# A two-layer encoder: where the memory keys are rounded first, which third of a group turns first, and in which order the last FFN unit multiplies

## The chip, the cores and the metric

The kernel runs on one core of one Trainium2 chip, as one launch. Its time is the device time of an execution in microseconds (us). The engines are named as in the profile: PE is TensorE (matmul and transpose by matmul), DVE is VectorE, ACT is ScalarE, POOL is GpSimd, and SP is SyncE, which here only issues DMA transfers. Each engine works through its own list of instructions strictly in order, and an instruction waits until what it reads and overwrites is free. A wait on one engine therefore also holds up everything behind it on that engine.

## The reference

A trunk of two layers on a sequence of 1,024 tokens with 1,024 channels, and 256 memory tokens, in float32:

```
mem_n = rmsnorm(mem, mem_norm_g)
for layer in (0, 1):
    u      = rmsnorm(h, norm_g[layer, 0])
    mem_kv = mem_n @ w_mem_kv[layer]
    if layer == 0:   # window attention: 16 query heads, 4 key/value heads of 64 channels,
                     # rotary, blocks of 128 tokens see one block to each side, a sink per head
        y = mixer_window_attn(u, mem_kv, a_w_in, a_sink, a_w_out, pos)
    else:            # a gated linear recurrence in both directions, 8 heads
        y = mixer_hgrn2(u, mem_kv, b_w_in, lb_fwd, lb_bwd, b_norm_g, b_w_out)
    # both mixers also hold 4 cross heads of 128 channels into mem_kv,
    # and project [own heads | cross heads] with one output matrix
    h = h + rmsnorm(y, norm_g[layer, 1])
    v = rmsnorm(h, norm_g[layer, 2])
    gate, up = split(v @ ffn_w_in[layer], 2)               # 1024 -> 2 x 2816
    f = (gelu(dwconv3(gate) + conv_b) * up) @ ffn_w_out[layer]
    h = h + rmsnorm(f, norm_g[layer, 3])
```

## The kernel before

Every float32 product is made of three matmuls on rounded halves: an operand x is kept as a rounded part xh and a rest xl, and the kernel adds xh·yh, xl·yh and xh·yl in PSUM (lines 81 to 83 in the mixers, line 555 in the FFN). Making the two parts is called `split`: ACT copies x to xh with rounding (line 86), then DVE subtracts xh from x (line 87). Where a weight is split the same pair stands at lines 76 and 77.

**Layer 0's mixer** works group by group, four groups g of four query heads with one key/value head. `proj(g)` projects eight tiles of 128 tokens (`token`, PE product `pj`, 24 matmuls each). DVE multiplies the result by the rotary cosines and sines (lines 278 and 279), ACT and DVE write the value `v` (lines 283 and 291). In group 0 the call also brings in three rows of the input, whose sums of squares ACT takes (line 290). `turn(b, ...)` transposes one half (four tiles) of queries and keys on PE into the PSUM tile `ptq` (line 303): three transposed parts w, of which w = 0 and 1 are queries (ACT lines 311 and 313, DVE 312 and 314 write `qs`) and w = 2 is the keys (ACT writes `kh` at line 86, DVE `kl` at line 87). `ptq` is one PSUM bank, so a part is transposed after the one before has been read.

`attend(g, ...)` then runs over eight blocks of 128 queries. For each of four heads PE makes scores `ps` from `qs` with `kh` and `kl` (lines 355 and 356), DVE adds the mask and takes the maximum (line 358), ACT takes the exponential (line 365). The last exponential of block n of group g is kept as `marks[g, n]`. After that the probabilities are scaled, transposed (`pt`, line 381), split (`ph`, `pl`) and multiplied with v (`po`, lines 384 and 385). Blocks 0 to 2 need only the first half of the keys, block 3 is the first that needs the second.

`cross_head(0, h, ...)` brings the memory keys and values of one cross head from DRAM into `kvl` (DMA on SP, line 186), and splits them into `kvh` and `kvl`. `cross_unit` uses them on PE, first at 162.7 us in the profiled execution.

After the fourth group the output projection starts. `wo0.begin` (line 420) reads the first heads' results back as `ul`, splits them (ACT line 449, DVE line 450) and multiplies by half of the output weights (`pb`, copied to `y0` by ACT at line 482). For tokens 6 and 7 the ACT copies of the read are held behind a mark:

```
wo0.begin(psq, ("pj", "pj", "ptq"), [...], {6: marks[3, 1], 7: marks[3, 1]})
```

**The FFN** of each layer multiplies in units of 128 hidden channels, f = 0 to 21. The 1,024 tokens are two halves; gate and up for two halves come from seven products instead of eight, numbered 1 to 7, each 12 matmuls (four steps of three). PSUM banks X, V and Y collect them: products 6, 7 and 4 are added one after the other to the same bank X, and before each next one ACT has to copy what X holds (`su`, then half `tj` of `g`, then half `ti` of `g`). Likewise V holds product 5 (copied to `s5`) and then 5 + 3. The right operands u6, u7 and u4 are made once for each layer by `operands()`, while `first_units` computes units 0 to 2. Unit 21 is made by `last_unit` (lines 711 to 732), which calls `ahead()` four times to load and split operands of the next stage, the second product of the FFN.

**What sets the order.** Nothing in the source is an explicit list: the program is given to a scheduler at build time, which orders every engine's instructions by priorities that follow the source. `tc.high_priority(AHEAD)` moves work up, and `tc.issue_after(x)` keeps the instructions within it behind the instruction x. A small edit therefore can move instructions at places that it does not name.

Of the kernel before, what the change touches and what calls it, by code (L numbers as in the profile page):

```python
# [8 lines left out]
F32 = mybir.dt.float32  # L9
# [4 lines left out]
ALU = mybir.AluOpType  # L14
# [4 lines left out]
P = 128  # L19
T = 1024  # L20
D = 1024
NT = T // P
# [22 lines left out]
AHEAD = 2000  # L45


def build(tc, A, out):
    nc = tc.nc
    act, dve, pool, pe = nc.scalar, nc.vector, nc.gpsimd, nc.tensor  # L50
# [18 lines left out]
    def wunit(src, n=1024, pl=None, eng=None):  # L69

        tg = ("wh", "wl") if pl is None else ("xwh", "xwl")
        h = (pl or ring).tile([P, 1024], F32R, tag=tg[0], name=tg[0])
        l = (pl or ring).tile([P, 1024], F32R, tag=tg[1], name=tg[1])
        raw = stg.tile([P, 1024], F32, tag="st", name="st")[:, :n]
        nc.sync.dma_start(raw, src)
        act.copy(h[:, :n], raw)  # L76
        (eng or dve).tensor_tensor(l[:, :n], raw, h[:, :n].bitcast(F32), op=ALU.subtract)  # L77
        return h, l
# [6 lines left out]
    def split(h, l, src):  # L85
        act.copy(h, src)  # L86
        dve.tensor_tensor(l, src, h.bitcast(F32), op=ALU.subtract)  # L87
# [91 lines left out]
                nc.sync.dma_start(kvd[l][:, :, 1, t * P:(t + 1) * P].rearrange("h p d -> p h d"),  # L179
                                  vm[:, t, :].rearrange("p (h d) -> p h d", h=4))  # L180

    def cross_head(l, h, wp):
        kvh = wp.tile([P, 2, 256], F32R, tag="kvh", bufs=1, name="kvh")
        kvl = wp.tile([P, 2, 256], F32R, tag="kvl", bufs=1, name="kvl")
        raw = kvl.bitcast(F32)
        nc.sync.dma_start(raw, kvd[l][h])
        split(kvh, kvl, raw)
        return *wunit(A["wxq"][l, h]), kvh, kvl

    def cross_unit(l, h, b, head, wp, tags, w0, pair):  # L190
# [44 lines left out]
    def window():  # L235
        ea = tc.alloc_tile_pool(name="attn0", bufs=1, reuse_waits="tile")
        ap_ = tc.alloc_tile_pool(name="attn", bufs=2, side="right", reuse_waits="tile")
        psq = tc.alloc_tile_pool(name="aps0", bufs=1, space=PSUM, reuse_waits="tile")
# [10 lines left out]
        xhead = [None]  # L249
# [6 lines left out]
        def proj(g):  # L256
# [5 lines left out]
            v = kvp.tile([P, NT, P], F32R, tag="v", bufs=1, name="v")  # L262
# [31 lines left out]

            def turn(b, rqs):
                hs = slice(b * 512, (b + 1) * 512)
                for w in range(3) if g or b else (2, 0, 1):
                    if g or b or w == 2:
                        tp = psq.tile([P, 4, P], F32, tag="ptq", bufs=1, name="ptq")
                    else:  # L300
                        tp = psp.tile([P, 4, P], F32, tag="pt", bufs=2, name="ptq")
                    for tt in range(4):
                        pe.transpose(tp[:, tt, :], rqs[tt][:, w * P:(w + 1) * P], ident)
                    tp = tp.rearrange("p a b -> p (a b)")
                    if w == 2:
                        split(kh[:, hs], kl[:, hs], tp)
                    else:
                        lo, hi = slice(0, 64), slice(64, 128)
                        q0, q1 = [ap_.tile([P, 512], F32R, tag="qs", bufs=8, name="qs") for _ in range(2)]
                        qs[2 * w][b], qs[2 * w + 1][b] = q0, q1  # L310
                        act.copy(q0[lo], tp[lo])
                        dve.tensor_tensor(q0[hi], tp[lo], q0[lo].bitcast(F32), op=ALU.subtract)
                        act.copy(q1[hi], tp[hi])
                        dve.tensor_tensor(q1[lo], tp[hi], q1[hi].bitcast(F32), op=ALU.subtract)
# [14 lines left out]
        marks, moved = {}, []  # L329
# [7 lines left out]
        def attend(g, qkv, blocks=range(NT)):  # L337
            qs, kh, kl, v = qkv
            for b in range(2):
                for nn in range(4):  # L340
# [5 lines left out]
                    o = pairs[0]  # L346
                    lo, hi = max(n - 1, 0), min(n + 2, NT)
                    w = (hi - lo) * P
# [55 lines left out]
                for _ in range(XU[g][b]):  # L404
                    xh_, xb_ = units.pop(0)
                    if xb_ == 0:
                        xhead[0] = cross_head(0, xh_, ea)
                    cross_unit(0, xh_, xb_, xhead[0], ap_, tags, ea, pair)

        dve.tensor_scalar_mul(sk8, sk, 8.0)  # L410
# [4 lines left out]
        ea.release()  # L415
        tables.release()
        attend(3, cur)
        wo0.open()
        y0 = wo0.w1.tile([P, NT, 512], F32, bufs=1, name="y0")
        wo0.begin(psq, ("pj", "pj", "ptq"), [y0[:, t, :] for t in range(NT)], {6: marks[3, 1], 7: marks[3, 1]})  # L420
        psp.release()
        ap_.release()

# [125 lines left out]
    def mmk(o, n, st, mv, first):  # L549

        for k in range(n):
            (ah, al), (bh, bl) = st(k), mv(k)
            new, end = first and k == 0, k == n - 1
            for x, y, e in ((ah, bh, False), (ah, bl, False), (al, bh, end)):
                pe.matmul(o, x, y, start=new, stop=e, skip_group_check=not first)  # L555
                new = False

    def ffn(l, wo, dst, gnext, halves_, out_halves):
        u2p = tc.alloc_tile_pool(name=f"u2{l}", bufs=1, reuse_waits="tile")
# [10 lines left out]
        ti, tj = hs(i), hs(j)  # L570
# [20 lines left out]
        def gtile():  # L591
            return fp.tile([P, T], F32, tag="g", bufs=1, name="g")
# [25 lines left out]
        def operands():  # L618

            xs = [fp.tile([P, 2, 512], F32, tag="c", bufs=3, name="c") for _ in range(2)]  # L620
            tmp = lambda: fp.tile([P, 2, 512], F32, tag="tt", bufs=2, name="tt")
            half = lambda x, kk: x[:, 2 * kk:2 * kk + 2]
            def more(o, x, part, kk, op):
                for c in range(2):
                    dve.tensor_tensor(o, x, half(part[c], kk).bitcast(F32), op=op)
                    x = o
            def out_of(sp, k, kk, x):
                sp(half(B[k][0], kk), half(B[k][1], kk), x)
            for kk, x in enumerate(xs):
                q = tmp()  # L630
                f32 = lambda t, c: half(t[c], kk).bitcast(F32)
                dve.tensor_tensor(x, f32(B[1], 0), f32(B[5], 0), op=ALU.subtract)
                dve.tensor_tensor(q, f32(B[1], 1), f32(B[5], 1), op=ALU.subtract)
                dve.tensor_tensor(x, x, q, op=ALU.add)
            for kk, x in enumerate(xs):
                out_of(split, 5, kk, x)
            yield
            for kk, x in enumerate(xs):
                more(x, x, B[3], kk, ALU.add)
                out_of(nsplit, 6, kk, x)  # L640
            yield
            for kk, x in enumerate(xs):
                q = tmp()
                more(q, x, B[1], kk, ALU.subtract)
                out_of(split, 7, kk, q)
            yield
            for kk, x in enumerate(xs):
                more(x, x, B[2], kk, ALU.subtract)
                out_of(split, 4, kk, x)
            yield  # L650
# [30 lines left out]
        def prod(k, w, ps, first):  # L681
            wh, wl = w
            bh, bl = B[k]
            mmk(ps, 4, lambda x: (wh[:, x * P:(x + 1) * P], wl[:, x * P:(x + 1) * P]),
                lambda x: (bh[:, x, :], bl[:, x, :]), first)


        oi, oj = (hs(b) for b in out_halves)
# [22 lines left out]
        def last_unit(w, x, v, y, s1, ahead):  # L711
            u = fp.tile([P, T], F32, tag="u", bufs=1, name="u")
            su = fp.tile([P, 512], F32, tag="su", bufs=1, name="su")
            s5 = fp.tile([P, 512], F32, tag="s5", bufs=1, name="s5")
            g = gtile()
            prod(6, w(6), x, False)
            act.copy(su, x)
            prod(2, w(2), y, True)
            dve.tensor_tensor(u[:, ti], y, s1, op=ALU.add)
            ahead()  # L720
            prod(7, w(7), x, False)
            act.copy(g[:, tj], x)
            prod(5, w(5), v, True)
            act.copy(s5, v)
            dve.tensor_tensor(g[:, tj], g[:, tj], s5, op=ALU.add)
            ahead()
            prod(4, w(4), x, False)
            act.copy(g[:, ti], x)
            ahead()
            prod(3, w(3), v, False)  # L730
            dve.tensor_tensor(u[:, tj], v, su, op=ALU.add)
            ahead()
            hidden(NF - 1, conv(NF - 1, g, u))

# [155 lines left out]
        y = {q: yp.tile([P, 4, 512], F32, name=q) for q in ("c11", "c21", "c12", "c22")}  # L890
# [5 lines left out]
        def rows(b, t):  # L896

            if gnext or b == ia:
                x = np_.tile([P, D], F32, tag="x", bufs=4 if gnext else 2, name="x")
            else:  # L900
                x = stg.tile([P, D], F32, tag="st", name="st")
            nc.sync.dma_start(x, h1d[l][tok(b, t), :])
            return x
# [31 lines left out]
        for k in SECOND:  # L935
            if k == 5:
                Xs = left()
            ps = Vs if k == 2 else Xs
            hold = []
            for p in range(NP2):  # L940
                while len(made) < 1:
                    second_ahead()
                h, l_ = made.pop(0)
# [5 lines left out]
                if k == 5 and p in (1, 3, 5, 7):  # L949
                    t = p // 2  # L950
                    tail(ia, t, y["c11"][:, t, :], ss["q11"][:, t:t + 1], y["c21"][:, t, :], ss["q21"][:, t:t + 1], rows(ia, t))
            if k == 3:
                last = [rows(ib, t) for t in range(4)]
            for t in range(4):
                if k in (1, 6, 7, 4):
                    act.copy(y[{1: "c11", 6: "c12", 7: "c22", 4: "c21"}[k]][:, t, :], ps[t])  # L956
                elif k in (2, 5):
                    q = y[{2: "c11", 5: "c22"}[k]][:, t, :]
# [461 lines left out]
    wo0 = Out(0, A["x"], "wout0", list(range(NT)))  # L1420
# [96 lines left out]
```

## Time and profile before

| | before |
|---|---|
| runs (us) | 2664.05, 2664.63, 2672.4; median 2664.63 |
| profiled execution | 2668.36 us, span 2666.4 us, granted clock 0.998 |
| PE busy | 2601.3 us, 98% of the span, 14,420 matmuls |
| DVE, ACT, POOL busy | 1813.5, 1378.9 and 473.7 us (68%, 52%, 18%) |
| end chain | PE 79%, DVE 12%, DMA 3%, ACT 3% |

A row of the timeline is: start, duration of one entry, engine, line, operation, output and input tiles, shape, count; in square brackets stands how long the engine was idle before it and what ended that. Matmuls overlap, so the time a matmul costs is the distance to the next one's start, not the duration shown. A row of waits is: who waited, for whom, microseconds in total, how many times, the longest. In the table by stretches the columns are the stretch, its length, the busy time of PE, PEld, DVE, ACT and POOL with counts, the granted PE clock, the share of DMA time and GB/s.

### The profile page before, as it was taken

What the parts mean: (1) busy time and instruction counts of PE and PEld (TensorE: products, weight loads), DVE (VectorE), ACT (ScalarE), POOL (GpSimd) and SP (SyncE); (2) the same over time, 40 slices, a digit from 0 to 9 for tenths busy, and PEclk for the clock granted to TensorE, in tenths of its full rate; (3) what the DMA queues carried; (4) which work ended last, traced back from release to release, by engine and by line L of the source; (5) the groups of instructions that cost most, each with busy time, mean ns of one, the idle gap of its engine ahead of it and who ended that gap; (6) DMA issues with size and microseconds to landing.
All of it is one profiled execution on the core that took longest, in us unless ns stands there. A gap on an engine that the chain in (4) does not pass through costs nothing.

```text
span 2666.4 us, 39108 instructions
## 1 busy us (share of the span) xinstructions
PE 2601.3 (98%) x14420; PEld 2185.9 (82%) x14420; DVE 1813.5 (68%) x3043; ACT 1378.9 (52%) x2503; POOL 473.7 (18%) x519
## 2 busy tenths in 40 slices
PE   8899999999999999999999999999999999999998
PEld 7888887788888887887888878888788788888887
DVE  6688786578655565478688686887757755656447
ACT  6477666445444444454455554555534444444443
POOL 0331010211111100031224131231211111110013
PEclk9999999999999999999999999999999999999999
DMA  9692232367777857674235251103436778774666
GB/s 353 232 190 54 74 97 72 109 184 194 198 203 192 210 145 258 192 249 154 83 110 149 81 125 56 52 25 96 140 125 176 188 200 210 197 206 158 224 191 237
DMA packets 195728, 425.93 MB, mean 160 GB/s; under 512 B 20048, under 2 KB 56272, under 8 KB 189904
## 3 DMA queue, kind: packets, MB, share of 16 engines
q1 hardware_dynamic: 161840, 325.11, 37.9%
q0 software_dynamic: 24544, 90.19, 16.3%
q10 hardware_dynamic: 9152, 8.14, 1.0%
q8 instruction: 113, 1.85, 0.3%
q14 instruction: 79, 0.65, 0.1%
HBM read 330.04 MB, written 116.39 MB: 167 GB/s over the span
## 4 chain that ended last, share of the span: by engine, by line
PE 79%; DVE 12%; DMA 3%; ACT 3%; issue 1%; POOL 1%; SPq 0%; ACTq 0%; DVEq 0%; POOLq 0%
PE X L555 28%; PE V L555 11%; PE pj L81 6%; PE pj L82 5%; PE pj L83 5%; PE Y L555 5%; PE pb L81 4%; PE pb L83 3%; PE pb L82 3%; DVE E L1139 1%; PE pt L381 1%; DVE wl L77 1%; DVE ER L1174 1%; DMA kvl<-kvd 1%; PE po L1242 1%
## 5 line engine op out<-in xcount | busy, mean ns | idle before, releaser
L87 DVE TENSOR_TENSOR wl<-st,wh 128x1024 fp32r<-128x1024 f32 (+1 forms) x238 | 262.8, 1111 | 325.3 <-ACT wh L86 285.2
L86 ACT CAST wh<-st 128x1024 fp32r<-128x1024 f32 (+1 forms) x238 | 222.5, 937 | 293.8 <-PE X L555 196.2
L81 PE MATMUL pj<-uh,wh 128*128 128x512 f32 x512 | 203.3, 397 | 3.7 <-DVE q L1084 2.0
L555 PE MATMUL X<-wl,wh 128*128 128x512 f32 x528 | 204.7, 389 | 0.0
L555 PE MATMUL X<-wh,wl 128*128 128x512 f32 x528 | 204.6, 389 | 0.0
L82 PE MATMUL pj<-ul,wh 128*128 128x512 f32 x512 | 201.7, 394 | 0.1
L83 PE MATMUL pj<-uh,wl 128*128 128x512 f32 x512 | 201.4, 394 | 0.0
L555 PE MATMUL X<-wh 128*128 128x512 f32 x528 | 198.7, 390 | 1.6 <-ACT c L956 1.6
L81 PE MATMUL pj<-wh,uh 128*128 128x384 f32 (+1 forms) x512 | 190.3, 373 | 9.4 <-DVE cos L1324 5.3
L82 PE MATMUL pj<-wl,uh 128*128 128x384 f32 (+1 forms) x512 | 187.2, 366 | 0.0
L83 PE MATMUL pj<-wh,ul 128*128 128x384 f32 (+1 forms) x512 | 187.1, 366 | 0.0
L77 DVE TENSOR_TENSOR wl<-st,wh 128x1024 fp32r<-128x1024 f32 (+1 forms) x92 | 117.4, 1281 | 28.9 <-ACT wh L76 28.3
L555 PE MATMUL V<-uh,wh 128*128 128x512 f32 x344 | 133.8, 389 | 0.0
L555 PE MATMUL V<-ul,wh 128*128 128x512 f32 x344 | 133.8, 389 | 0.0
L555 PE MATMUL V<-uh,wl 128*128 128x512 f32 x344 | 133.8, 389 | 0.0
L76 ACT CAST wh<-st 128x1024 fp32r<-128x1024 f32 (+1 forms) x98 | 98.9, 1015 | 46.6 <-PE pj L82 25.2
L555 PEld LDWEIGHTS X<-wh 128*128 128x128 f32 x528 | 99.1, 188 | 22.5 <-ACT c L956 2.0
L555 PEld LDWEIGHTS X<-wl,wh 128*128 128x128 f32 x528 | 99.1, 188 | 20.6
L555 PEld LDWEIGHTS X<-wh,wl 128*128 128x128 f32 x528 | 99.1, 188 | 20.6
L81 PEld LDWEIGHTS pj<-uh,wh 128*128 128x128 f32 x512 | 96.3, 188 | 24.0 <-DVE q L1084 2.9
L81 PEld LDWEIGHTS pj<-wh,uh 128*128 128x128 f32 x512 | 96.6, 189 | 21.0 <-issue 5.5
L925 POOL TENSOR_TENSOR c<-c,g 128x512 f32<-128x512 f32 x24 | 43.8, 1844 | 392.4 <-PE X L555 163.0
(399 smaller groups left out, 7211.5 us busy)
## 6 DMA issues: line engine op xcount, KB each, us to landing
st<-hid SPq DMA_DIRECT2D x154, 256.0 KB, 3.1
st<-in_ffw_dram SPq DMA_DIRECT2D x108, 256.0 KB, 3.2
w2s<-in_ffw_dram POOLq DMA_DIRECT2D x24, 1024.0 KB, 8.5
st<-in_ffw_dram SPq DMA_DIRECT2D x46, 512.0 KB, 4.2
hid<-tt SPq DMA_DIRECT2D x88, 256.0 KB, 4.7
st<-w2s SPq DMA_DIRECT2D x88, 256.0 KB, 3.2
sx<-in_ffw_dram SPq DMA_DIRECT2D x84, 256.0 KB, 4.0
sy<-in_ffw_dram SPq DMA_DIRECT2D x42, 512.0 KB, 6.9
```

The costliest lines, as they stand in the source:

```text
L76: act.copy(h[:, :n], raw)
L77: (eng or dve).tensor_tensor(l[:, :n], raw, h[:, :n].bitcast(F32), op=ALU.subtract)
L81: pe.matmul(o, ah, bh, start=first, stop=False)
L82: pe.matmul(o, ah, bl, start=False, stop=False)
L83: pe.matmul(o, al, bh, start=False, stop=last)
L86: act.copy(h, src)
L87: dve.tensor_tensor(l, src, h.bitcast(F32), op=ALU.subtract)
L381: pe.transpose(tp[:, j, :], sm[:, j, c * P:(c + 1) * P], ident)
L555: pe.matmul(o, x, y, start=new, stop=e, skip_group_check=not first)
L925: pool.tensor_tensor(y[q][:, t, :], y[q][:, t, :], g3[:, c], op=ALU.mult)
L1139: dve.tensor_tensor_scan(B[:, rev], smask, a_[:, rev], 0.0, op0=ALU.mult, op1=ALU.add)
L1174: dve.tensor_tensor(re_, re_, bc(pl_[:, :, e:e + 1], [P, nb, n]), op=ALU.mult)
```

## The change

Four places change the program, a fifth is a shift of priority.

1. `cross_head` takes a mark. For the first cross head of layer 0 the ACT copy of the memory keys (`kvh`, now line 188) is issued behind `marks[0, 3]`, the last exponential of group 0's block 3; the DVE subtraction (line 189) follows it. The transfer of `kvl` is issued where it was.
2. In the last group's second half, `turn` transposes the keys before the queries (order 2, 0, 1).
3. The reads for tokens 6 and 7 in the output projection stand behind `marks[3, 2]` instead of `marks[3, 1]`.
4. `last_unit` gives its products in the order 2, 6, 5, 7, 3, 4, and `issue_after` ties 5 behind 6, 3 behind 7 and 4 behind 3. Before, the source had 6, 2, 7, 5, 4, 3 without ties and the scheduler placed 2, 5, 6, 3, 7, 4, with product 4 of the unit before between 5 and 6.
5. The split of the operand u7 in `operands()` gets high priority.

```
-    def cross_head(l, h, wp):
+    def cross_head(l, h, wp, behind=None):
...
-        split(kvh, kvl, raw)
+        with tc.issue_after(behind.ins) if behind else nullcontext():
+            act.copy(kvh, raw)
+        dve.tensor_tensor(kvl, raw, kvh.bitcast(F32), op=ALU.subtract)
...
-                for w in range(3) if g or b else (2, 0, 1):
+                for w in range(3) if (g, b) not in ((0, 0), (3, 1)) else (2, 0, 1):
...
-                        xhead[0] = cross_head(0, xh_, ea)
+                        xhead[0] = cross_head(0, xh_, ea, None if xh_ else marks[0, 3])
...
-        wo0.begin(..., {6: marks[3, 1], 7: marks[3, 1]})
+        wo0.begin(..., {6: marks[3, 2], 7: marks[3, 2]})
...
-                out_of(split, 7, kk, q)
+                with tc.high_priority(AHEAD):
+                    out_of(split, 7, kk, q)
...
-            prod(6, w(6), x, False)
-            act.copy(su, x)
             prod(2, w(2), y, True)
             dve.tensor_tensor(u[:, ti], y, s1, op=ALU.add)
             ahead()
-            prod(7, w(7), x, False)
+            done = prod(6, w(6), x, False)
+            act.copy(su, x)
+            with tc.issue_after(done.ins):
+                prod(5, w(5), v, True)
+            act.copy(s5, v)
+            ahead()
+            done = prod(7, w(7), x, False)
             act.copy(g[:, tj], x)
-            prod(5, w(5), v, True)
-            act.copy(s5, v)
             dve.tensor_tensor(g[:, tj], g[:, tj], s5, op=ALU.add)
+            with tc.issue_after(done.ins):
+                done = prod(3, w(3), v, False)
+            dve.tensor_tensor(u[:, tj], v, su, op=ALU.add)
             ahead()
-            prod(4, w(4), x, False)
+            with tc.issue_after(done.ins):
+                prod(4, w(4), x, False)
             act.copy(g[:, ti], x)
-            ahead()
-            prod(3, w(3), v, False)
-            dve.tensor_tensor(u[:, tj], v, su, op=ALU.add)
             ahead()
             hidden(NF - 1, conv(NF - 1, g, u))
```

The order of instructions shows where the work went. In the changed kernel line numbers are 2 to 7 higher behind line 181, so line 285 there is line 283 before. First ACT in group 0's projection, before:

```order
L283 ACTIVATE v<-pj,rs_86 128x64 x2
L290 ACTIVATE row,xss<-row 128x1024 x2
L86 CAST kvh<-kvl 128x512
L283 ACTIVATE v<-pj,rs_86 128x64
L290 ACTIVATE row,xss<-row 128x1024
L283 ACTIVATE v<-pj,rs_86 128x64 x2
L311 CAST qs<-ptq 64x512
```

and after, the same place:

```order
L285 ACTIVATE v<-pj,rs_86 128x64 x2
L292 ACTIVATE row,xss<-row 128x1024 x2
L285 ACTIVATE v<-pj,rs_86 128x64
L292 ACTIVATE row,xss<-row 128x1024
L285 ACTIVATE v<-pj,rs_86 128x64
L313 CAST qs<-ptq 64x512
```

The cast of `kvh` is gone from between the values of tokens 1 and 2. On ACT after, it stands 48 rows further on, among the exponentials of blocks 3 and 4 of group 0:

```order
L367 ACTIVATE sm,su<-sm,nm 128x384 x4
L188 CAST kvh<-kvl 128x512
L365 ACTIVATE es<-es 128x4
L367 ACTIVATE sm,su<-sm,nm 128x384 x3
L365 ACTIVATE es<-es 128x4
```

The subtraction on DVE follows it there. Second, ACT in the last group's second half, before:

```order
L311 CAST qs<-ptq 64x512
L387 COPY o<-po 64x4x128
L313 CAST qs<-ptq 64x512
L365 ACTIVATE sm,su<-sm,nm 128x384 x4
L449 CAST uh<-ul 128x6x128 x2
L86 CAST kh<-ptq 128x512
L76 CAST xwh<-st 128x1024 x2
L482 COPY y_5184<-pb 128x512 x2
L363 ACTIVATE es<-es 128x4
```

and after, the same work from the cast of the keys on:

```order
L86 CAST kh<-ptq 128x512
L367 ACTIVATE sm,su<-sm,nm 128x256
L365 ACTIVATE es<-es 128x4
L367 ACTIVATE sm,su<-sm,nm 128x256 x3
L376 ACTIVATE sm<-sm,rd 128x256 x2
L313 CAST qs<-ptq 64x512
L86 CAST ph<-pt 128x512 x2
L315 CAST qs<-ptq 64x512
L389 COPY o<-po 64x4x128
L367 ACTIVATE sm,su<-sm,nm 128x384 x4
L313 CAST qs<-ptq 64x512
L76 CAST xwh<-st 128x1024 x2
```

The keys' cast moved from behind block 1's exponentials (384 wide) to ahead of block 0's (256 wide). The two read casts of tokens 6 and 7 (`uh<-ul` with 6x128, line 451 there), which stood in front of it, moved down to seven rows below the last row shown, behind block 2's exponentials. Third, ACT at the end of layer 0's first FFN stage, before:

```order
L842 COPY g<-X 128x512
L584 ACTIVATE c<-g,cb,ncw 128x1024
L717 COPY su<-X 128x512
L86 CAST wh<-st 128x1024
L587 ACTIVATE c<-c 128x1024
L86 CAST wh<-st 128x1024
L722 COPY g<-X 128x512
L86 CAST wh<-st 128x1024
L728 COPY g<-X 128x512
```

and after:

```order
L849 COPY g<-X 128x512
L587 ACTIVATE c<-g,cb,ncw 128x1024
L724 COPY su<-X 128x512
L727 COPY s_9330<-V 128x512
L590 ACTIVATE c<-c 128x1024
L86 CAST wh<-st 128x1024
L730 COPY g<-X 128x512
L86 CAST wh<-st 128x1024 x2
L738 COPY g<-X 128x512
```

The copy of `g` behind product 7 (line 722, now 730) still stands behind one weight cast. On PE, the products 7 and 4 of the last unit, which stood next to each other,

```order
L555 MATMUL X<-u7h,wh 128x512
L555 MATMUL X<-u7l,wh 128x512
L555 MATMUL X<-u7h,wl 128x512
L555 MATMUL X<-u4h,wh 128x512
L555 MATMUL X<-u4l,wh 128x512
```

now have the twelve matmuls of product 3 (into V) between them, of which the last three stand here:

```order
L557 MATMUL V<-uh,wh 128x512
L557 MATMUL V<-ul,wh 128x512
L557 MATMUL V<-uh,wl 128x512
L557 MATMUL X<-u4h,wh 128x512
L557 MATMUL X<-u4l,wh 128x512
```

The product 4 moved back by one product. The rows of the two u7 splits stand where they stood. Beyond these places the order of all engines differs in many rows from the middle of group 0 to the end of layer 0's output projection, and in units 0 to 5 of layer 0's FFN.

More of the change, by code (lines that the diff above doesn't have):

```diff
@@ L419, in window @@
         y0 = wo0.w1.tile([P, NT, 512], F32, bufs=1, name="y0")
-        wo0.begin(psq, ("pj", "pj", "ptq"), [y0[:, t, :] for t in range(NT)], {6: marks[3, 1], 7: marks[3, 1]})
+        wo0.begin(psq, ("pj", "pj", "ptq"), [y0[:, t, :] for t in range(NT)], {6: marks[3, 2], 7: marks[3, 2]})
         psp.release()
@@ L554, in mmk @@
             for x, y, e in ((ah, bh, False), (ah, bl, False), (al, bh, end)):
-                pe.matmul(o, x, y, start=new, stop=e, skip_group_check=not first)
+                last = pe.matmul(o, x, y, start=new, stop=e, skip_group_check=not first)
                 new = False
+        return last
     def ffn(l, wo, dst, gnext, halves_, out_halves):
@@ L683, in prod @@
             bh, bl = B[k]
-            mmk(ps, 4, lambda x: (wh[:, x * P:(x + 1) * P], wl[:, x * P:(x + 1) * P]),
-                lambda x: (bh[:, x, :], bl[:, x, :]), first)
+            return mmk(ps, 4, lambda x: (wh[:, x * P:(x + 1) * P], wl[:, x * P:(x + 1) * P]),
+                       lambda x: (bh[:, x, :], bl[:, x, :]), first)
         oi, oj = (hs(b) for b in out_halves)
```

## The prediction

> **What bounds the kernel now.** I read the page's first two parts, then PE's waits, then the timeline around the long ones.
>
> ```profile
> PE 2601.3 (98%) x14420; PEld 2185.9 (82%) x14420; DVE 1813.5 (68%) x3043; ACT 1378.9 (52%) x2503; POOL 473.7 (18%) x519
> PE pj L81 <- DVE cos L1324: 5.3, 1, 5.3
> PE ps L355 <- ACT kh L86: 3.2, 2, 2.6
> PE X L555 <- ACT g L722: 2.8, 2, 1.4
> PE X L555 <- ACT c L956: 1.6, 1, 1.6
> 100.00:395.00 295.00, 282.16 (x1629) 251.08 (x1628) 238.27 (x644) 209.34 (x529) 54.18 (x70) 1.00 0.45 115
> ```
>
> PE is busy 2601.3 of 2666.4 us, so PE sets the time and no edit that leaves its matmuls alone can win more than the 65.1 us in which it idles, plus what it loses at a lower clock. The change removes no matmul. Three of the waits shown are what its edits touch: 5.3, 2.6 and twice 1.4 us. In the last row (a stretch of the attention) PE is busy 282.16 of 295 us: 12.8 us of small waits, many of which now stand in another order.
>
> **Memory keys.** The chain that ended last passes through one transfer:
>
> ```profile
> 64.02 14.01 DMA kvl<-kvd
> 78.05 0.62 ACT L86 CAST kvh<-kvl 128x512 fp32r<-128x512 f32 x1 [6.55 <-DMA kvl<-kvd]
> 78.57 0.31 ACT L283 ACTIVATE v<-pj,rs 128x64 fp32r<-128x64 f32 x1
> 78.70 0.69 DVE L87 TENSOR_TENSOR kvl<-kvl,kvh 128x512 fp32r<-128x512 f32 x1 [6.61 <-ACT kvh L86]
> 79.31 0.28 DVE L291 SCALAR_TENSOR_TENSOR v<-pj,rs,v 128x64 fp32r<-128x64 f32 x1
> 73.58 0.82 PE L303 MATMUL ptq<-ident,rq 128*128 128x128 f32 x6
> 79.73 0.66 PE L81 MATMUL pj<-wh,uh 128*128 128x384 f32 x1 [5.33 <-DVE cos L1324]
> 81.15 0.52 PE L82 MATMUL pj<-wl,uh 128*128 128x384 f32 x1
> 81.47 0.52 PE L83 MATMUL pj<-wh,ul 128*128 128x384 f32 x1
> 83.59 0.34 PE L82 MATMUL pj<-wl,uh 128*128 128x384 f32 x1
> 83.76 0.33 PE L83 MATMUL pj<-wh,ul 128*128 128x384 f32 x1
> 79.64:83.05 3.41, 3.32 (x10) 3.35 (x11) 1.51 (x8) 0.59 (x3) 2.14 (x4) 0.50 0.00 0
> 162.68 0.39 PE L81 MATMUL ps<-kvh,xh 128*128 128x256 f32 x1
> L290 ACT ACTIVATE row<-row x3: 1045/1059/1064, 69.1 to 78.8; 128x1024 f32<-128x1024 f32 x3
> DMA to landing us min/median/max: 6.5/7.3/10.1
> ```
>
> The transfer takes 14.01 us; ACT and DVE both sit with their lists behind it (6.55 and 6.61 us idle), so token 2's value, which needs nothing of it, is written at 78.57 and 79.31, the PSUM bank comes free, and PE starts the next token at 79.73 after 5.33 us. PE then runs 3.41 us at clock 0.50: matmuls 0.32 us apart (81.15 to 81.47) instead of 0.17 (83.59 to 83.76), ten of them, 10 x 0.15 = 1.5 us. Nothing reads the keys before 162.68.
>
> In the order of after, ACT writes token 2's value directly behind the second input row, and the cast is among group 0's later exponentials, some 60 us on. SP issues the transfer at its old place, and nothing is queued behind it on SP that is due. What is late next? The third input row: its ACT square (1.06 us, the row of line 290) stands between the values of tokens 2 and 3, and token 3's value is needed only when PE has finished one more token, 24 x 0.17 = 4.1 us. I take the whole gap and the clock loss: -5.3 - 1.5 = -6.8 us. The ends: 0 if another input of token 2's value were late (DVE and ACT show 6.6 us of idleness with nothing else in it, so I don't believe this), -6.8 at most.
>
> [...]
>
> The moved pair costs ACT 0.62 and DVE 0.69 us at its new place. PE waits for these engines there in small steps, such as this one, just behind the new place:
>
> ```profile
> 136.94 0.60 ACT L365 ACTIVATE sm<-sm,nm 128x384 f32<-128x384 f32 x1
> 141.56 0.44 PE L355 MATMUL ps<-kh,qs 128*128 128x384 f32 x1 [0.39 <-DVE mx L358]
> ```
>
> Bounds 0 and 1.3 us; I take +0.4, by that row.
>
> **Keys first, and the reads a block later.** The rows of group 3's second half:
>
> ```profile
> 413.61 1.55 ACT L449 CAST uh<-ul 128x768 fp32r<-128x768 f32 x2
> 415.18 0.59 ACT L86 CAST kh<-ptq 128x512 fp32r<-128x512 f32 x1
> 415.82 1.01 PE L355 MATMUL ps<-kh,qs 128*128 128x384 f32 x2 [2.60 <-ACT kh L86]
> 417.75 0.63 PE L81 MATMUL pb<-wh,uh 128*128 128x512 f32 x1
> 418.17 0.63 PE L82 MATMUL pb<-wl,uh 128*128 128x512 f32 x1
> 421.54 0.40 PE L82 MATMUL pb<-wl,uh 128*128 128x512 f32 x1
> 421.78 0.39 PE L83 MATMUL pb<-wh,ul 128*128 128x512 f32 x1
> 413.26 0.62 DVE L358 CUSTOM_DVE_ANT_0 sm<-ps,wmask,sk 128x384 f32<-128x384 f32 x1
> 414.46 1.83 DVE L450 TENSOR_TENSOR ul<-ul,uh 128x768 fp32r<-128x768 f32 x2 [0.17 <-ACT uh L449]
> 410.73:414.15 3.42, 1.62 (x8) 0.83 (x8) 3.19 (x12) 2.95 (x9) 0.00 (x0) 1.00 0.00 0
> 414.10:421.00 6.90, 5.07 (x12) 3.88 (x13) 6.64 (x14) 6.88 (x16) 0.00 (x0) 0.51 0.24 78
> ```
>
> The keys' cast stands behind the read casts of tokens 6 and 7 (1.55 us), PE waits 2.60 us, and then runs at half clock until 421: 0.42 us between `pb` matmuls (417.75 to 418.17) against 0.24 later, for some eight of them, 1.5 us; with four score matmuls up to 2.4. So 5.0 us is the most to win here.
>
> But DVE is busy 3.19 of 3.42 us and 6.64 of 6.90 in the two stretches: it, and not the wait, sets the pace. What changes is which of its work comes first. The reads (1.83 us) and the keys' subtraction (about 0.69) leave the stretch; three more score scans (0.62 each) and one query subtraction (as wide as the keys', 0.69) enter it ahead of the `pb` products, 2.55 us for 2.5. So PE reaches the first `pb` at about 417.7 as before, but with three more heads' scores behind it: six matmuls 384 wide at 0.17 us, 1.0 us, rounded up to -1.3 for a slow stretch that may be shorter. Ends: 0 and -5.0. The held reads are needed by the last two tokens' products, after 36 `pb` matmuls (8.2 us), so I cost the later mark at nothing; without that cover it is 1.55 + 0.9 us.
>
> [...]
>
> **Last FFN unit.** In both layers:
>
> ```profile
> 998.95 1.05 ACT L86 CAST wh<-st 128x1024 fp32r<-128x1024 f32 x1 [0.71 <-PE X L555]
> 999.90 0.58 ACT L722 COPY g<-X 128x512 f32<-128x512 f32 x1
> 1000.54 0.50 PE L555 MATMUL X<-u4h,wh 128*128 128x512 f32 x1 [1.39 <-ACT g L722]
> 2446.26 0.50 PE L555 MATMUL X<-u4h,wh 128*128 128x512 f32 x1 [1.39 <-ACT g L722]
> 1035.04 0.50 PE L555 MATMUL X<-wh 128*128 128x512 f32 x1 [1.57 <-ACT c L956]
> ```
>
> Product 4 adds to the bank that the copy must read first, and the copy stands behind a weight cast. With product 3 between them PE has twelve 512-wide matmuls of other work (12 x 0.24 = 2.9 us), more than cast and copy (0.95 + 0.58 = 1.5). The same holds at 6 -> 5 -> 7: `su` is copied while 5 runs, although it now stands behind the bias activation of unit 20's convolution. -1.39 a layer, -2.8 us; ends 0 and -2.8, since the wait of 1.57 us at 1035.04 may take a part of layer 0's.
>
> **FFN's first units and the rest.** The u7 splits stand where they stood, so part 5 does nothing itself; the order of units 1 to 5 changes around it.
>
> ```profile
> 634.84 0.50 PE L555 MATMUL Y<-uh,wl 128*128 128x512 f32 x1 [0.53 <-DVE wl L87]
> ```
>
> This wait goes, and a wait for a copy of `g` (0.58 us plus its queue) comes: +0.3, bounds -0.5 and +1. For the attention's 12.8 us of small waits in another order I take 0, with -4 and +6 (a third less, half more).
>
> **The sum**: -6.8 + 0.4 - 1.3 - 2.8 + 0.3 = -10.2 us. The profiled execution took 2668.36 us (span 2666.4 and 2.0 around it), so the sum gives 2658.2 against it; it lies 3.7 us above the median of 2664.63, from which I get 2654.4.
>
> **The rivals.**
> - The reordered attention gives it back. Every queue differs from group 0 on, and in 100 to 395 DVE is busy 238.27 of 295 us, so a list in another order can wait more. At +6, with the keys part at 0 and the pair at 1.3, it is -10.2 + 6 + 1.3 + 0.9 = -2.0: 2662.6. For it: most waits are single DVE or ACT instructions of 0.2 to 1.4 us. Against: the same scheduler made both orders by the same rules.
> - Everything is won: the keys part gives 5.0, its wait and its slow stretch both gone: -10.2 - 3.7 = -13.9, 2650.7. For it: both causes of the 2.60 us wait (late transpose, reads ahead) are taken away. Against: DVE is 93 to 96% busy there.
> - Slower: DVE becomes the bound of the attention. If each of the order's new waits put as much work before the awaited instruction as the 2.60 us row does, seven or eight such waits (7 x 2.60 = 18.2 us) would exceed the gain by 0.3%: 2664.6 - 10.2 + 18.2 = 2672.6. It decides from 12.8 us of small waits growing to 31. Nothing in the profile shows it; the one such row is removed.
> - The change doesn't do what it says: token 2's value stays late because an input row ahead of it on ACT is, and the last unit's wait moves to 1035.04. Then -10.2 + 6.8 + 1.4 = -2.0, 2662.6. Against it: the input rows land 6.5 to 10.1 us after their issue just before 64.02, so by 74, and ACT had done two of them before its idle time.
>
> **How the numbers follow.** About 8 us, 0.3%, is what a measurement can tell from no change. My forecast, 2654.4 with 2650 to 2657, has 0.47; everything won 0.16; attention gives it back 0.22; not what it says 0.08; slower 0.07. The first two are faster but for a rim of the first above 2656.6: 0.60. Within 0.3% lie the rim and the third and fourth: 0.32. Slower 0.08, with a little of the rest. The low end adds the attention's -4 to the case in which all is won, 2646.5; the high end, 2665, is the sum of all bounds against me without the slower case.
>
> **What would show it.** Right: PE's wait for `cos` near 74 us gone and no slow clock until 84; the wait for `kh` near 413 gone, with several waits for `mx` or `qs` of under 1 us in its place; no wait for `g` at the end of either FFN stage, 1.57 us still before the line of `c`. Wrong: a gap over 2 us near 74; PE idle in 100 to 395 above 19 us; a new wait in the last unit for `su` or `s5`.

## The result and the profile after

The changed kernel takes 2663.39 us in the median of 22 runs (2660.27 to 2674.21), the kernel before, run beside it, 2668.72 (22 runs, 2664.05 to 2673.0). The ratio is 0.9983, with a 95% interval of 0.9977 to 0.9989: 4.5 us faster. The forecast was 10.2 us. (The forecast started from three runs of before, of which two are the lowest of the 22: their median was 2664.63.)

The page of the changed kernel, its first row and three of PE's waits (engine, line, for whom: total us, times, longest):

```profile
PE 2601.1 (98%) x14420; PEld 2184.7 (82%) x14420; DVE 1818.5 (68%) x3043; ACT 1378.5 (52%) x2503; POOL 469.6 (18%) x519
PE ps L357 <- DVE mx L360: 8.9, 14, 1.5
PE po L387 <- DVE pl L87: 3.3, 5, 1.2
PE X L557 <- ACT c L963: 0.9, 1, 0.9
```

PE's work is the same to 0.2 us. The waits for `cos`, for `kh` (2.60 us) and for `g` are gone from the list. In their place the wait for `mx`, the row maximum that DVE writes for each score, has grown from 3.6 to 8.9 us; its row before was:

```profile
PE ps L355 <- DVE mx L358: 3.6, 6, 1.4
```

The timeline of the changed kernel at the places that the prediction spoke of, ACT and PE near 72 us, then PE in group 3's second half, then PE and ACT at the end of layer 0's first FFN stage:

```profile
72.34 0.31 ACT L285 ACTIVATE v<-pj,rs 128x64 fp32r<-128x64 f32 x1 [0.62 <-DVE xss L1328]
74.83 1.06 ACT L292 ACTIVATE row<-row 128x1024 f32<-128x1024 f32 x1 [2.18 <-DMA row<-in_x_dram]
73.71 0.49 PE L305 MATMUL ptq<-ident,rq 128*128 128x128 f32 x3
73.96 0.42 PE L81 MATMUL pj<-wh,uh 128*128 128x384 f32 x1
...
416.46 0.44 PE L357 MATMUL ps<-kh,qs 128*128 128x384 f32 x1 [0.82 <-DVE mx L360]
417.45 0.39 PE L81 MATMUL pb<-wh,uh 128*128 128x512 f32 x1
417.68 0.40 PE L82 MATMUL pb<-wl,uh 128*128 128x512 f32 x1
...
994.05 1.05 ACT L86 CAST wh<-st 128x1024 fp32r<-128x1024 f32 x1 [0.95 <-PE X L557]
995.01 0.58 ACT L730 COPY g<-X 128x512 f32<-128x512 f32 x1
996.57 0.39 PE L557 MATMUL V<-uh,wl 128*128 128x512 f32 x1
996.80 0.39 PE L557 MATMUL X<-u4h,wh 128*128 128x512 f32 x1
1030.46 0.50 PE L557 MATMUL X<-wh 128*128 128x512 f32 x1 [0.86 <-ACT c L963]
```

All three mechanisms work. Token 2's value is written at 72.34 instead of 78.57 and PE goes on at 73.96 without a wait. The `pb` products start at 417.45, with `kh` no longer in the way. Product 4 follows product 3 without a break, and the copy of `g`, still behind a weight cast, ends 1.2 us before it is needed.

To see where the time went, compare the start of the same matmul in both. The gain at the 48th `pj<-wh,ul` (89.8 us before) is 6.9 us. The 51st matmul `V<-uh,wl`, in layer 0's FFN, is a point behind all that the attention and the output projection do; its row in the kernel before and in the changed kernel:

```profile
720.63 0.39 PE L555 MATMUL V<-uh,wl 128*128 128x512 f32 x1
```

```profile
718.45 0.39 PE L557 MATMUL V<-uh,wl 128*128 128x512 f32 x1
```

Of 6.9 us, 2.2 are left. The table by stretches shows the loss, from the end of the stall to group 3's last projection, before (84 to 396 us) and after (77 to 396); columns: length, busy time of PE, PEld, DVE, ACT, POOL, granted clock, DMA share, GB/s:

```profile
84.00:396.00 312.00, 299.16 (x1729) 267.81 (x1728) 251.03 (x680) 216.05 (x541) 62.81 (x84) 1.00 0.46 119
```

```profile
77.00:396.00 319.00, 300.77 (x1727) 268.38 (x1727) 258.00 (x684) 215.12 (x541) 62.73 (x86) 0.99 0.45 119
```

PE started this stretch 7 us earlier and ended it at the same time. It idled 319 - 300.77 = 18.2 us instead of 12.8, 5.4 more, and the clock was below 1.00 in one piece:

```profile
152.54:155.95 3.41, 1.33 (x8) 0.72 (x6) 3.35 (x9) 2.17 (x5) 2.07 (x3) 1.00 1.04 216
155.95:159.36 3.41, 3.30 (x9) 2.92 (x10) 3.35 (x13) 1.89 (x7) 0.00 (x0) 0.50 1.06 211
154.69 0.39 PE L357 MATMUL ps<-kh,qs 128*128 128x256 f32 x1 [0.84 <-DVE mx L360]
156.06 0.58 PE L357 MATMUL ps<-kh,qs 128*128 128x256 f32 x1 [0.87 <-DVE mx L360]
```

DVE is busy 3.35 of 3.41 us there, PE 1.33, and nine matmuls at clock 0.50 follow. The 512 wide ones start 0.42 us apart (157.68 to 158.10) instead of 0.23, the 384 wide ones 0.32 (158.42 to 158.74) instead of 0.17 (159.73 to 159.90): by my estimate from these distances about 1.5 us of loss. So the freed time was given back in the attention, a stretch that the diff doesn't name. Most of it went early: up to 225 us, which is group 0 and the first half of group 1, PE idled 8.5 us instead of 3.7, so 4.8 of the 5.4 us stand there.

### The profile page after: what moved, and what is told of

Its sections match the earlier page's. It is cut to its first block, busy times and chain, and to the rows that moved or that the text cites. A ratio compares the mean times of both kernels' runs of the same rounds, so it can differ in the third digit from the quotient of the medians.

```text
span 2659.7 us, 39101 instructions
## 1 busy us (share of the span) xinstructions
PE 2601.1 (98%) x14420; PEld 2184.7 (82%) x14420; DVE 1818.5 (68%) x3043; ACT 1378.5 (52%) x2503; POOL 469.6 (18%) x519
## 4 chain that ended last, share of the span: by engine, by line
PE 82%; DVE 10%; ACT 3%; DMA 3%; issue 1%; POOL 1%; SPq 0%; ACTq 0%; DVEq 0%; POOLq 0%
PE X L557 29%; PE V L557 11%; PE pj L81 6%; PE pj L82 6%; PE pj L83 6%; PE Y L557 5%; PE pb L81 4%; PE pb L83 4%; PE pb L82 4%; DVE E L1146 1%; PE po L1249 1%; PE pt L383 1%; DVE ER L1181 1%; PE pt L116 1%; PE pu L1225 1%
## 5 line engine op out<-in xcount | busy, mean ns | idle before, releaser
L83 PEld LDWEIGHTS pj<-uh,wl 128*128 128x128 f32 x512 | 96.2, 188 | 18.7
```

The source lines that it names most:

```text
L83: pe.matmul(o, al, bh, start=False, stop=last)
```

## The experiments

The theory: taking the pair (the cast of `kvh` and the subtraction) from its place makes the scheduler lay out the attention in another order, and this order costs what the stall cost. The first rival: the stretch has a pace of its own (DVE, or the transfers), so that a start 7 us earlier is worth nothing in any order. The second: the pair at its new place costs the time. In every kernel but two the attention's order differs; in "all but the keys' cast" and "last unit alone" it is that of before up to the output projection. Edit 5 was not run alone. The kernel without the first edit has it and the one with the last unit alone has not, and from 500 us on these two have the same rows in the same order on PE, DVE, ACT and POOL; so edit 5 moved nothing there.

**The first edit alone.**

```
+        with tc.issue_after(behind.ins) if behind else nullcontext():
+            act.copy(kvh, raw)
...
+                        xhead[0] = cross_head(0, xh_, ea, None if xh_ else marks[0, 3])
```

> The changed kernel's trace has the 5.33 us wait near 74 us gone, PE 7.3 us ahead at 85 us, and this lead lost again between 77 and 314 us (waits 12.7 instead of 7.7 us, and a stretch of 3.41 us at half clock from 156 us). Only the first edit is in this kernel. If this edit alone gives the lead away again, by the order that it leads to, then the time is that of before within 2 us (ratio 0.9993 to 1.0007), with the lead gone by 314 us here too. If the other edits are needed for the loss, it is faster by 5 to 7 us (ratio 0.9975 to 0.998).

Measured: 2666.82 us against 2668.02, ratio 0.9998 (0.9989 to 1.0007). Its lead at the 48th `pj<-wh,ul` is 7.2 us, and at the point in the FFN it is behind:

```profile
721.38 0.39 PE L557 MATMUL V<-uh,wl 128*128 128x512 f32 x1
77.00:397.00 320.00, 302.24 (x1728) 269.94 (x1727) 257.89 (x684) 214.92 (x541) 62.20 (x85) 0.99 0.45 118
PE ps L357 <- DVE mx L360: 6.3, 10, 1.5
```

So this edit removes the stall and is worth nothing measurable, without any help of the others. (The row of waits is for 77 to 397 us; before, for 84 to 396, it is 2.7 us in 5 waits.)

**All but the first edit.**

```
-        with tc.issue_after(behind.ins) if behind else nullcontext():
-            act.copy(kvh, raw)
-        dve.tensor_tensor(kvl, raw, kvh.bitcast(F32), op=ALU.subtract)
+        split(kvh, kvl, raw)
```

> Edits 2 to 5 without the first: the order of groups 0 to 2 is that of before, the wait near 74 us stays. If the net gain of the changed kernel comes from these edits alone: 5 to 6 us faster (ratio 0.9977 to 0.9982), of which 2.5 to 3 us by 430 us, 1.4 to 1.7 us in each FFN stage's end. If they are worth what the forecast gave them (1.3 + 2.8 - 0.3): 3.8 us faster (ratio 0.9986).

Measured: 2664.09 against 2668.02, ratio 0.9983 (0.9975 to 0.9992): 4.5 us, the whole gain of the change. This lies between the two expectations and does not tell them apart. In its profile 1.25 us are gained by the point in the FFN, up to which only edits 2 and 3 have moved rows, and no stretch at half clock follows in group 3.

**The last unit alone.** The fourth edit as in the change, of which these lines are the core:

```
-            prod(6, w(6), x, False)
-            act.copy(su, x)
             prod(2, w(2), y, True)
...
+            with tc.issue_after(done.ins):
+                done = prod(3, w(3), v, False)
...
+            with tc.issue_after(done.ins):
+                prod(4, w(4), x, False)
```

> Edit 4 alone. By the forecast 2.8 us faster (1.39 us in each layer, ratio 0.9990). By the changed kernel's trace 3.4 to 4.1 us (1.69 us in each layer, and 0.7 us more at the wait for the copy c behind layer 0's first FFN stage, ratio 0.9985 to 0.9987).

Measured: 2665.47 against 2668.02, ratio 0.9990 (0.9981 to 0.9999), 2.7 us; the two expectations lie too close for the interval. In the profiles of this kernel and of the changed one, the lead grows by 1.69 us across each of the two waits. That is 0.3 more than PE's idle time of 1.39: before, the starts around the first wait are 1.79 us apart (998.75 to 1000.54) where 0.23 is the distance without a wait, and the next ones are 0.33 and 0.24 apart. The wait for `c` is no part of this gain: it is 0.7 us here and 0.86 in the changed kernel (row at 1030.46 above), but over all profiles 0.7 to 2.4 us in the ten with edit 4 and 1.0 to 1.6 in the four without it.

**The cast behind other blocks, and the transfer ahead.** All other edits are in; only the mark differs (`marks[0, 0]` as shown, or block 2 or 5), or the cast stays unheld and the transfer is raised:

```
-        xhead[0] = cross_head(0, xh_, ea, None if xh_ else marks[0, 3])
+        xhead[0] = cross_head(0, xh_, ea, None if xh_ else marks[0, 0])
...
+        with tc.high_priority(AHEAD) if l + h == 0 else nullcontext():
+            nc.sync.dma_start(raw, kvd[l][h])
```

> The changed kernel with the keys' cast behind block 0's last exponential instead of block 3's. The stall near 74 us is gone here too, but the attention's order is another one. If the order is what gives the lead away, the lead left at 314 us (7.3 us at 85 us) is different from the changed kernel's (which had none left, 0.3 us behind) by 2 us or more, and the time with it: 2656 to 2661 where the order is luckier. If another engine or the transfers set the pace of this stretch whatever the order, the lead at 314 us is gone again within 1 us and the time is the changed kernel's, 2663 +- 1.

> The changed kernel with the keys' cast behind block 2 of group 0: a fourth order of the attention, without the stall. The lead on the kernel before is read when ACT writes the last value of group 3's projection (395.82 us before): 0.3 us behind in the changed kernel, 3.5 us ahead with the cast behind block 0. If the order decides, this order leaves another lead, anywhere from 0 to 7 us, with waits between 77 and 314 us that differ accordingly (12.7 us in the changed kernel, 11.3 behind block 0, 7.7 before). If the stretch has a pace of its own that no order beats, the lead is again 0 to 3.5 us and the waits 11 us or more.

> As the run before, with the cast behind block 5, only just before the keys are needed: a fifth order. Same two readings: the lead at group 3's last value anywhere from 0 to 7 us if the order decides, 0 to 3.5 us with 11 us of waits or more if the stretch has its own pace.

> The stall is taken away in another manner: the cast keeps its place in the source, unheld, and the transfer of the keys is issued at high priority, ahead of the input rows. If the transfer then lands before ACT comes to it (by 72 us) the wait near 74 us is gone or under 1 us; lead at 85 us of 5 to 7 us. If the order decides, its own order leaves 0 to 7 us of that at group 3's last value. If the lead was lost because of the moved pair (0.62 us on ACT, 0.69 on DVE among the attention's blocks), it keeps 1.3 us more than the others.

Measured: block 0: 2662.51 us, ratio 0.9981 (0.9972 to 0.9990). Block 2: 2656.43, ratio 0.9958 (0.9944 to 0.9973). Block 5: 2662.82, ratio 0.9976 (0.9966 to 0.9986). Transfer ahead: 2662.38, ratio 0.9979 (0.9970 to 0.9989). The stall is gone in all of them (leads of 6.1 to 7.0 us at the 48th `pj<-wh,ul`), and what is left of it at the FFN ranges from 3.2 to 7.6 us (table below). The transfer ahead, with the pair in its place in the source, keeps 5.2 us: less than block 2, where the pair is moved, and more than the other two, so the pair's new place is not what decides. By time only block 2 stands out: the intervals of the other three hold the changed kernel's 0.9983. Block 0's time is even the one that a pace of the stretch's own would give (2663 +- 1), and block 5, 2.0 us ahead at group 3's last value, fits that reading too. Block 2 does not: 5.5 us ahead there, and 9.6 us of waits between 77 and 314 us.

**Block 2, the first edit alone; block 2 again with all edits; block 2 without the third edit.**

```
-                        xhead[0] = cross_head(0, xh_, ea)
+                        xhead[0] = cross_head(0, xh_, ea, None if xh_ else marks[0, 2])
...
-        wo0.begin(..., {6: marks[3, 2], 7: marks[3, 2]})
+        wo0.begin(..., {6: marks[3, 1], 7: marks[3, 1]})
```

> The first edit alone, with the cast behind block 2 instead of block 3. With block 3 this edit alone was worth nothing (ratio 0.9998). If the order of the attention decides what the freed 7.3 us are worth, this kernel is faster than before by 5 to 8 us (ratio 0.997 to 0.998), with PE's waits between 77 and 314 us near 9.5 us instead of 12.4. If the edit is worth nothing by itself, and only together with the others, the ratio is 0.999 to 1.0005.

> The kernel with the cast behind block 2 and all other edits, measured again with more runs, since the first time gave only four (2655.7 to 2661.5 us). Expected 2656 to 2659 us, 9 to 12 us faster than before (ratio 0.9955 to 0.9968). Its profile shows the same order; where it has another number of stretches of 3.41 us at half clock than the four of the first profile (310, 361, 1027 and 1918 us), the lead differs by 1.2 to 1.9 us for each.

> The kernel with the cast behind block 2, without the third edit: the reads for tokens 6 and 7 stand behind block 1 again (keys still first). If the later reads are what makes the keys' edit worth its 1.3 to 1.8 us, the lead gained between 396 and 600 us is 1 to 2 us smaller here and the time 1 to 2 us longer than with the edit. If not, the times agree within 1 us.

Measured: the cast alone, 2664.10 against 2668.94, ratio 0.9983 (0.9974 to 0.9992), just short of the expected range. All edits again, 2656.76, ratio 0.9960 (0.9947 to 0.9973). That is as expected. Without the third edit, 2659.45, ratio 0.9966 (0.9953 to 0.9979): what the later reads are worth is not told apart from nothing. From the cast alone, the same two readings as of the first experiment:

```profile
713.51 0.39 PE L557 MATMUL V<-uh,wl 128*128 128x512 f32 x1
77.00:396.00 319.00, 305.90 (x1752) 272.08 (x1751) 256.88 (x695) 218.07 (x543) 66.33 (x89) 0.99 0.45 120
PE ps L357 <- DVE mx L360: 1.2, 2, 0.8
```

One number in the call, 2 for 3, and PE is busy 305.90 of the 319 us in which it was busy 300.77 in the changed kernel; the waits for `mx` are 1.2 us, and the lead, 6.4 us behind the stall, is 7.1 in the FFN. This is one profiled execution, and the fastest of this kernel (2660.22); over all runs the cast behind block 2 alone is worth 4.5 us by the ratio, and its interval overlaps that of the cast behind block 3 alone (0.9989 to 1.0007) by 0.0003. With all edits the two places are clearly apart: 0.9958 and 0.9960 for block 2, both below 0.9974 with their intervals, against 0.9983 (0.9977 to 0.9989) for block 3.

**The sums later.** None of the five edits; the weight sums on POOL's queue start three tokens later:

```
-                sum_steps[0].send(done)
+                if g or t >= 3:
+                    sum_steps[0].send(done)
```

> The kernel before with none of the five edits, but the weight sums of layer 0 start three tokens later, so that their first three transfers (1 MB each) do not run beside the keys' transfer of 14 us. If the transfers' crowd is what made the keys late, the keys' transfer lands in 8 us or less and the wait near 74 us falls from 5.33 us to under 1. What that is worth at the end depends on the order of the attention that comes with it: a lead of 0 to 7 us at group 3's last value if the order decides.

Measured: 2660.88 against 2668.94, ratio 0.9970 (0.9961 to 0.9980), 8.0 us. Its keys' transfer, the longest of them, its cast on ACT, and the two readings:

```profile
DMA to landing us min/median/max: 2.5/3.2/8.0
72.36 0.60 ACT L86 CAST kvh<-kvl 128x512 fp32r<-128x512 f32 x1
712.06 0.39 PE L556 MATMUL V<-uh,wl 128*128 128x512 f32 x1
77.00:390.00 313.00, 300.49 (x1733) 269.49 (x1732) 255.82 (x685) 216.48 (x539) 67.86 (x89) 0.99 0.48 127
```

The transfer takes 8.0 us instead of 14.0, the cast runs at 72.36 with no idle time before it, there is no wait, and the whole lead is kept: 7.2 us behind the stall, 8.6 in the FFN. The crowd of transfers was the main cause of the late keys: in the eleven profiles with the sums and the transfer in their old places it takes 12.7 to 14.0 us, in the two with the sums later 8.0 and 9.7. And the stall was worth its full price in an order that does not take it back. A kernel in the changed kernel's order with the first three sums cut to a 32nd has no time on record, so what these transfers do to the pace of one and the same order is not shown.

**The sums later and edits 2 to 5, without the first.** On the changed kernel:

```
-                sum_steps[0].send(done)
+                if g or t >= 3:
+                    sum_steps[0].send(done)
...
-        with tc.issue_after(behind.ins) if behind else nullcontext():
-            act.copy(kvh, raw)
-        dve.tensor_tensor(kvl, raw, kvh.bitcast(F32), op=ALU.subtract)
+        split(kvh, kvl, raw)
```

> The weight sums three tokens later, and edits 2 to 5 of the change without the first. Its order up to group 3 is that of the run with the sums later alone, which kept the whole lead (9.5 us at group 3's last value). If the parts add up: 8.0 us from there and 4.5 us from edits 2 to 5, together 12.5 us less than before's 2668.5, about 2656 (ratio 0.9953). If the order of the output projection that comes with it gives a part back, 2658 to 2660.

Measured: 2658.39 against 2667.88, ratio 0.9960 (0.9948 to 0.9972), 10.7 us. The time is in the second range, a part given back, but the interval holds 0.9953 as well. This kernel and the one with all edits and the cast behind block 2 are faster than the kernel before and the changed one; the two are not told apart. In the profile its lead at group 3's last value is 5.9 us where 9.5 was expected, although up to there its rows stand in the same order as with the sums later alone: it met half clock in three pieces on the way instead of one.

The table puts the readings together. Lead is on before's profile, in us, at the 48th `pj<-wh,ul` and at the 51st `V<-uh,wl`; "idle" is PE's idle time from 77 us (84 in the three kernels that keep the stall: before, all but the cast, last unit alone) to group 3's last value, by the same view as the rows above; "slow" counts the pieces of 3.41 us at half clock between 85 and 720 us.

| kernel | lead 90 us | lead 720 us | idle | slow | ratio |
|---|---|---|---|---|---|
| before | | | 12.8 | 2 | |
| changed (block 3) | 6.9 | 2.2 | 18.2 | 1 | 0.9983 |
| block 3 alone | 7.2 | -0.7 | 17.8 | 5 | 0.9998 |
| all but the cast | 0.0 | 1.25 | 13.4 | 0 | 0.9983 |
| last unit alone | -0.9 | -1.7 | 13.0 | 3 | 0.9990 |
| block 0, all | 7.0 | 4.2 | 15.1 | 2 | 0.9981 |
| block 5, all | 6.7 | 3.2 | 15.7 | 2 | 0.9976 |
| transfer ahead, all | 6.1 | 5.2 | 13.4 | 1 | 0.9979 |
| block 2 alone | 6.4 | 7.1 | 13.1 | 2 | 0.9983 |
| block 2, all | 6.7 | 7.6 | 12.9 | 2 | 0.9958 |
| block 2, all, again | 7.2 | 7.6 | 13.0 | 2 | 0.9960 |
| block 2, reads as before | 6.7 | 7.8 | 12.9 | 2 | 0.9966 |
| sums later alone | 7.2 | 8.6 | 12.5 | 2 | 0.9970 |
| sums later, edits 2 to 5 | 6.7 | 5.2 | 12.6 | 4 | 0.9960 |

The first rival falls: the same start leaves 13 or 18 us of idle time by the order. Profiles that share the order of this stretch agree in it within 0.6 us (before and the next two with its order, 12.8 to 13.4; block 3, 17.8 and 18.2; the four of block 2, 12.9 to 13.1; sums later, 12.5 and 12.6). The leads are less steady, and so is the number of pieces at half clock in one and the same order of this stretch (1 and 5 for block 3, 2 and 4 for the sums later), so a difference of 3 or 4 us between the leads of two single profiles ranks nothing. Nor does the idle time explain every row: the transfer ahead idles 13.4 us, hardly more than block 2, and its ratio is 0.9979; why is open. Which rows of the order make the difference is not shown either: the orders differ from each other in hundreds of rows. What is shown is whom PE waits for in the bad one (`mx`).

## Why the prediction was right or wrong

It was wrong in size: 4.5 us measured, 10.2 forecast. The sign held, and so did the range: 2663.39 lies 1.6 us under its top, although the low first runs put the whole range about 4 us too low. The top of 2665 itself doesn't follow from the terms: all bounds against the forecast add to +8.3 us (2672.9), and to +1.5 (2666.1) if the keys' 6.8 us are kept. The low end, by the terms, is 2646.7.

- **Memory keys, -6.8: the mechanism right, and at its place it was worth 6.1 to 7.2 us** in the eleven profiles without the stall. The third input row was late (its square at 74.83), and harmless, as argued.
- **The step that failed: "For the attention's 12.8 us of small waits in another order I take 0".** It was +5.4 us of waits and a new piece at half clock (about 1.5), together the 6.9 us won. The bound was +6, so the size was foreseen and given too small a weight: this is the prediction's first rival (2662.6 us, chance 0.22). In the prediction's own window, 100 to 395 us, PE idled 17.9 us instead of 12.8, so its sign of being wrong, more than 19, was set too high to speak. Its argument against, that the same scheduler made both orders, says nothing about which of them is better; six orders without the stall gave 12.5, 12.9, 13.4, 15.1, 15.7 and 18.2 us of idle time. None came near the 8.8 us of the lower bound: 0 was the favourable edge and not the middle.
- **The moved pair, +0.4:** not told apart. The cast ran at 136.53 us on ACT and the subtraction at 137.17 on DVE as placed.
- **Keys first, -1.3: near in size, for a reason half right.** PE reached the first `pb` at 417.45 (forecast 417.7) with the scores ahead; 1.25 us by the profile without the first edit, 1.8 by the ratios (4.5 - 2.7), whose intervals overlap, so the runs alone don't tell it from nothing. The half clock, for which the forecast put in no more than the rounding from 1.0 to 1.3 us, mostly stayed away (1.00 from 414.1 to 421 us in the changed kernel, 0.51 before): between 405 and 425 us all five profiles without this edit have one to three pieces of it, of the nine with it two have one piece each (at 412 us, block 2 with the reads as before and the last kernel). With the sums later there is one such piece both without edits 2 to 5 and with them, and there they gained almost nothing up to the FFN: from group 3's last value on, the lead falls by 0.9 us without them (9.5 to 8.6) and by 0.7 with them (5.9 to 5.2). So what this edit is worth seems to be mainly the slow pieces that it saves; few profiles show it.
- **Last unit, -2.8: right.** Measured 2.7 by the ratio, by the profiles 2 x 1.69 = 3.4; the interval holds both. The wait for `c` behind layer 0's stage stayed, as argued. The `su` and `s5` copies came in time.
- **FFN's first units, +0.3:** the two waits are 0.25 and 0.60 us instead of 0.27 and 0.53: nothing.
- **"The change doesn't do what it says"** fell; so did the slower case.

## What to carry to other kernels

An edit that frees an engine at one place in a kernel whose order is made at build time is two edits: the stall removed, and a new order behind it; here the second cost between nothing and all that the first had won. So try a few equivalent places for the moved work and read each over the whole reordered stretch, not at the place of the edit; PE's idle time there was steadier here than the lead of a single profile. And when a transfer is late because others crowd it (14.0 us before, 8.0 with the sums later), moving the crowd can be better than moving the one who waits for it, as here with the order that came along.

## What the runs showed of the hardware

In the kernel before, PE idled 5.33 us up to 79.73, and the clock was 0.50 from 79.64 to 83.05. It halved behind shorter gaps too. In the row 152.54 to 155.95 above PE is busy 39% (1.33 of 3.41 us), no gap is over 0.87 us, and 3.41 us at 0.50 follow. From 1913.81 in the same profile PE is busy 1.17 of 3.42 us, with one gap of 2.25 us, and 3.41 us at 0.50 follow from 1917.23. Before, PE is busy 1.62 of 3.42 us (47%) from 410.73, its longest gap is 2.60 us, and it is at 0.50 from 414.15 to 420.97. It was not so each time: before, PE is busy 1.58 of 3.41 us (46%) from 72.81 and 1.76 of 3.41 (51%) from 1919.42, and both times the next 3.41 us are at 1.00. What decides between these is not shown.

Before, the clock fell at 79.64 and at 414.15 us, which is 334.51 us or 98 times 3.413 apart; in the changed kernel at 155.95 and at 1917.23, 1761.28 us or 516 times 3.413 apart. The two profiles of the kernel with the cast behind block 2 and all edits have the same order, the same lead in the FFN (7.56 and 7.57 us), and end 6.8 and 11.6 us ahead of before. The first, with 2661.53 us, met half clock at four places, one of them at 1027 us, behind the point where the leads agree; its clock over the whole span is 0.997, that of the second 0.998. By the expectation one piece is worth 1.2 to 1.9 us, so one is only a part of the 4.8 us between the two. The spread within one kernel (2653.65 to 2661.53 us for this one) is of the size of a few such pieces; that they explain it was not shown.
